# First stretch of a two-layer decoder trunk: the first column pair of x and its weights loaded in halves, the first split by halves of the tokens, fewer products of ones, another order of products

## The chip, the cores and the metric

The kernel runs on one core of one Trainium2 chip. The metric is the device time of one execution in microseconds (us), as the median of several runs.

Engines are named as the profile names them. PE is TensorE, the matrix engine, and PEld its weight loader, which puts the stationary operand of each product into the array. DVE is VectorE, ACT is ScalarE, POOL is GpSimd. SP is SyncE, which here only issues DMA transfers. SBUF is the on-chip memory from which the engines read; PSUM is the memory into which PE writes.

## The reference, cut to what matters

The program is two decoder layers over 512 tokens of width 1024, in 32-bit floats: attention with a short convolution in the first, gated linear attention in the second, each with a gated MLP and a per-layer embedding. The change lies in the first 20 us, where the first layer's input projection begins:

```python
h = _rms_norm(x, mix_norm[i])
q, k, v, cb, cc, cx = _split(h @ w_in, HY_SPLITS)      # 512, 128, 128, 512, 512, 512 columns
q = _apply_rope(_rms_norm(q.reshape(b, s, ATTN_Q_HEADS, HEAD_DIM), q_norm), cos, sin)
k = _apply_rope(_rms_norm(k.reshape(b, s, ATTN_KV_HEADS, HEAD_DIM), k_norm), cos, sin)
```

Keys and values together are 256 columns of `w_in` (512 to 767). They are the first products that the kernel makes.

## The kernel before

**Products in three.** PE multiplies 32-bit operands in a rounded form (fp32r). To keep precision each operand is split in two: ACT rounds it to a high part (lines 112 and 146), and DVE subtracts that from the original for the low part (lines 113 and 147). `mm3` (lines 166 to 168) makes high times high, high times low and low times high. So every product needs ACT's result first and then DVE's, and three matmuls on PE.

**The first stretch** is the start of `mixer0`. Activations are worked on transposed: features on the 128 partitions, tokens along the row. The 1024 features are eight blocks of 128, called columns here, m or k = 0 to 7. For each column PE transposes four blocks of 128 x 128, one for each group of 128 tokens t (line 477), into a 512-wide PSUM tile (`ps`). ACT and DVE read that tile, multiply it with the gain of the norm (the column `vec`) and split it into an operand pair (`operand`, lines 112 and 113). They also copy the plain tile into `xT[m]` for later (`keep`, line 492: even columns on ACT, odd ones on DVE). The weights of keys and values for two columns at a time are split by `weight` (lines 146 and 147, 512 wide). `keys_values(k)` then makes twelve products 256 columns wide: four token groups times the three of `mm3`, added up in two PSUM tiles (`pa`) over k = 0 to 7.

**Loads.** SP issues, for each of four pairs of columns, two transfers of x (256 tokens by 256 columns each, 256 KB, into `xin[0]` and `xin[1]`, line 441) and one of the weights (256 KB into `kvr`, line 442), one after another. ACT issues the identity matrix and the gains of the norms (lines 191 and 217). POOL's transfers come later: they wait for the last column of x to land.

**Products of ones.** `idle(n)` (line 202) makes n products of a matrix of ones, 512 columns wide, whose result goes nowhere. There are seven ahead of the first transposes, and three between the first transposes and the first product. Between the first transposes stands one more small product, which turns the gains of the norm into columns (line 226; DVE copies them out, line 227).

**What sets the order.** Around the change, PE, DVE and ACT follow the order in which the code is written (`manual_schedule`); each engine works its own list strictly in that order, and an instruction that waits holds up everything behind it on its engine. Behind that stretch a scheduler orders the instructions. The order in the code is: transposes of columns 0 and 1, products of ones, weights 0, operands 0 and 1, products of k = 0; then for c = 1 to 3: transposes of columns 2c and 2c + 1, the two copies into xT for the pair before, the operands and weights of this pair, and the products of k = c. The products of k = 4 to 7 follow. After them come the products of the queries, 512 wide (lines 166 to 168 into `ps`), whose weights are loaded by SP and split by ACT and DVE 1024 wide.

Of the kernel before, what the change touches and what calls it, by code (L numbers as in the profile page):

```python
# [18 lines left out]
P = 128  # L19
S = 512  # L20
D = 1024
NT = S // P
ND = D // P
# [33 lines left out]
class Kernel:  # L57
# [121 lines left out]
    def setup(self):  # L179
        nc, a = self.nc, self.a  # L180
        self.mhalf = self.cp.tile([P, 32], F32, name="mhalf")[:, :16]
        self.cf = self.cp.tile([P, P + 64 + 256], F32, name="cf")
        self.ident = self.cf[:, :P]
        ones = self.sq()[:, :P]
        self.ones_r = self.cp.tile([P, P], F32R, name="ones_r")
        self.nowhere = self.pa()
        with self.tc.manual_schedule(engines={ET.PE, ET.DVE, ET.Activation}):
            nc.vector.memset(ones, 1.0)
            nc.vector.tensor_copy(self.ones_r, ones)
            nc.vector.memset(self.mhalf, -0.5)  # L190
            nc.scalar.dma_start(self.ident, a["cst_f"][:, :P])
            self.vec0 = self.load_vectors0()
            self.idle(7)
        self.ones = self.ones_r.bitcast(F32)
        self.invf = self.cf[:, P + 32 : P + 64]
        self.amask = self.cf[:, P + 64 :]
# [233 lines left out]
    def mixer0(self):  # L430
        nc, a, tc = self.nc, self.a, self.tc
        with tc.tile_pool(name="m0", bufs=1) as mp:
            w_in = a["hy_w_in"][0].rearrange("(k p) n -> p k n", p=P)
            self.xT = [self.xp.tile([P, S], F32, name=f"xT{m}") for m in range(ND)]
            xin = [mp.tile([P, 2, D], F32, tag="s", name=f"xin{u}", bufs=2) for u in range(2)]
            kvr = self.raw(ND, 256)
            for c in range(4):
                cols = slice(c * 256, (c + 1) * 256)
                for u in range(2):
                    rows = a["x"][0, u * 256 : (u + 1) * 256, cols]  # L440
                    nc.sync.dma_start(xin[u][:, :, cols], rows.rearrange("(t p) d -> p t d", p=P))
                nc.sync.dma_start(kvr[:, 2 * c : 2 * c + 2, :], w_in[:, 2 * c : 2 * c + 2, 512:768])
            self.gate = xin[1][:, 1, D - 1 :]
            self.late(self.cf[:, P + 32 : P + 33])
            nc.gpsimd.dma_start(self.cf[:, P + 32 :], a["cst_f"][:, P:])
# [1 line left out]
            xg = self.xg = []  # L447
            tok = lambda k, t: (xg[k][0][:, t * P : (t + 1) * P], xg[k][1][:, t * P : (t + 1) * P])
            pkv = [self.pa() for _ in range(2)]
            pkv = [pkv[t // 2][:, (t % 2) * 256 : (t % 2) * 256 + 256] for t in range(NT)]  # L450
            wkv = []

            def keys_values(k):
                for t in range(NT):
                    self.mm3(
                        pkv[t], tok(k, t), wkv[k // 2](k % 2, 0, 256),
                        start=k == 0 and t % 2 == 0, stop=k == ND - 1 and t % 2 == 1,
                    )

            def first_keys_values():  # L460
                mm = nc.tensor.matmul
                wh, wl = wkv[0](0, 0, 256)
                for t in range(NT):
                    xh, _ = tok(0, t)
                    mm(pkv[t], xh, wh, start=t % 2 == 0, stop=False)
                    mm(pkv[t], xh, wl, start=False, stop=False)
                for t in range(NT):
                    mm(pkv[t], tok(0, t)[1], wh, start=False, stop=False)

            def turned_in(c):  # L470
                pss = [self.ps() for _ in range(2)]
                for u in range(2):
                    if c == 0 and u == 1:
                        self.vec0()
                    for m, ps in zip((2 * c, 2 * c + 1), pss):
                        for t in (2 * u, 2 * u + 1):
                            nc.tensor.transpose(
                                ps[:, t * P : (t + 1) * P], xin[u][:, t % 2, m * P : (m + 1) * P], self.ident
                            )
                return pss  # L480

            def weight(c):
                wkv.append(self.cut(kvr[:, 2 * c : 2 * c + 2, :], "a", (48, 16)))

            def operand(m, ps):
                hl = self.pair(self.fp, "a0", "a1")
                self.split(hl, ps, self.g_mix[0][:, m : m + 1])
                xg.append(hl)

            def keep(c, pss):  # L490
                return [
                    copy(self.xT[2 * c + u], pss[u]) for u, copy in enumerate((nc.scalar.copy, nc.vector.tensor_copy))
                ]

            with tc.manual_schedule(engines={ET.PE, ET.DVE, ET.Activation}):
                pss = turned_in(0)
                self.idle(3)
                weight(0)
                for u in range(2):
                    operand(u, pss[u])  # L500
                first_keys_values()
                for c in range(1, 4):
                    ahead = turned_in(c)
                    keep(c - 1, pss)
                    pss = ahead
                    operand(2 * c, pss[0])
                    weight(c)
                    operand(2 * c + 1, pss[1])
                    keys_values(c)
                last = keep(3, pss)  # L510
                for k in range(4, ND):
                    keys_values(k)
            wq = [self.weights(w_in[:, k0 : k0 + 4, :512], 4, 512, by="a") for k0 in (0, 4)]
            sums = self.few(NT, "ss")
            junk = mp.tile([P, D], F32, tag="pT", name="junk")
# [174 lines left out]
            pss = {}  # L690
# [4 lines left out]
            def conv_w(nme, j2):  # L695
                c0 = starts[nme] + 256 * j2
                return self.weights(w_in[:, :, c0 : c0 + 256], ND, 256)

            def conv_halves(nme, j2, *ins):
                c0 = starts[nme] + 256 * j2  # L700
                raw = self.raw(ND, 256)
                nc.sync.dma_start(raw, w_in[:, :, c0 : c0 + 256])
                ws = []

                def half(*ins):
                    c = slice(len(ws) * P, len(ws) * P + P)
                    with ExitStack() as es:
                        for x in ins:
                            es.enter_context(tc.issue_after(x))
                        ws.append(self.cut(raw[:, :, c], "b"))  # L710

                half(*ins)
                return (lambda k, a, b: ws[a // P](k, 0, P)), half
# [36 lines left out]
            w = conv_w("x", 0)  # L750
# [4 lines left out]
            w = conv_w("c", 0)  # L755
# [9 lines left out]
            w, second = conv_halves("b", 0, copied["q", 1])  # L765
# [7 lines left out]
            w, second = conv_halves("x", 1, copied[0, 1], begun[1])  # L773
# [9 lines left out]
            w, second = conv_halves("c", 1, copied[1, 1], begun[2])  # L783
# [5 lines left out]
            w, second = conv_halves("b", 1, copied[2, 1], begun[3])  # L789
# [1372 lines left out]
```

## Time and profile before

| | |
|---|---|
| Median of 3 runs | 1194.47 us (1193.74 to 1194.7) |
| Profiled execution, its own time | 1194.58 us |
| Its span, from the first to the last recorded instruction | 1192.8 us |
| Instructions | 17964 |
| Busy: PE, DVE, ACT, POOL | 1187.1, 994.6, 685.4, 43.1 us |
| DMA | 117.62 MB, mean 99 GB/s |

The profile is one execution of the program, recorded by the chip. A row of its timeline gives the start and the duration in us, the engine, the line of the code, the operation, what it writes and reads, the shapes and, in brackets, how long the engine sat idle just before and what released it. A matmul's recorded duration contains the way through the array. Matmuls overlap in it, so PE's pace is read from the distance between two starts, not from the durations. A transfer's "us to landing" counts from its issue. Names such as `wh`, `wl`, `a`, `ps`, `pa` are tiles: the high and the low part of the weights, the operands, the two kinds of PSUM tile.

### The profile page before, as it was taken

Reading aid. Unit: us, or ns where it says so; the run is one execution under the profiler, and the core shown is the slowest. Engines: PE = TensorE matmul, PEld = TensorE weight load, DVE = VectorE, ACT = ScalarE, POOL = GpSimd, SP = SyncE. Lnnn points to the kernel's source line nnn. Section 1 sums busy time; section 2 is a strip of 40 time slices with the busy share of each in tenths; the row PEclk is TensorE's granted clock in tenths of the full one; section 3 lists DMA queues with packets and bytes.
Section 4 is the critical chain, followed back from the end, with each engine's and each line's share of the span. In section 5 each row is a group of like instructions: output and inputs, shape, how many; then the busy total and the mean of one; then the engine's idle time right before and its main releaser. Section 6 shows DMA issues by size and latency. Waiting matters only on the chain.

```text
span 1192.8 us, 17964 instructions
## 1 busy us (share of the span) xinstructions
PE 1187.1 (100%) x7121; PEld 1038.9 (87%) x7121; DVE 994.6 (83%) x1571; ACT 685.4 (57%) x1116; POOL 43.1 (4%) x64
## 2 busy tenths in 40 slices
PE   9999999999999999999999999999999999999998
PEld 8887789999998889989988988889999999899887
DVE  6787687899999987789779866687999999986895
ACT  7566465655565744566563654555555656644764
POOL 2600000000000000000100000000000000000000
PEclk9999999999999999999999999999999999999999
DMA  7213322424232333232412222323242423423601
GB/s 224 82 62 91 90 71 71 142 71 142 71 118 95 119 129 98 97 106 70 142 60 71 74 69 71 107 65 112 72 141 71 142 72 122 135 89 98 212 1 71
DMA packets 110856, 117.62 MB, mean 99 GB/s; under 512 B 2824, under 2 KB 105794, under 8 KB 110772
## 3 DMA queue, kind: packets, MB, share of 16 engines
q1 hardware_dynamic: 109936, 115.88, 29.8%
q8 instruction: 56, 0.92, 0.3%
q0 software_dynamic: 560, 0.42, 0.3%
q14 instruction: 28, 0.23, 0.1%
q10 hardware_dynamic: 276, 0.18, 0.1%
HBM read 114.37 MB, written 2.10 MB: 98 GB/s over the span
## 4 chain that ended last, share of the span: by engine, by line
PE 100%; DVE 0%; ACT 0%; issue 0%
PE ps L166 14%; PE ps L167 14%; PE ps L168 14%; PE pa L167 7%; PE pa L166 7%; PE pa L168 7%; PE ps L912 6%; PE ps L914 6%; PE ps L913 6%; PE pa L912 2%; PE pa L914 2%; PE pa L913 2%; PE ps L1527 1%; PE ps L1526 1%; PE ps L1525 1%; PE pa L1866 1%
## 5 line engine op out<-in xcount | busy, mean ns | idle before, releaser
L146 ACT ACTIVATE wh<-raw 128x1024 fp32r<-128x1024 f32 (+4 forms) x144 | 143.6, 999 | 94.9 <-PE ps L167 61.7
L147 DVE TENSOR_TENSOR wl<-raw,wh 128x1024 fp32r<-128x1024 f32 (+4 forms) x144 | 166.0, 1153 | 28.9 <-ACT wh L146 28.1
L857 ACT ACTIVATE wh<-raw 128x1024 fp32r<-128x1024 f32 x84 | 89.3, 1063 | 119.6 <-DVE raw L881 63.8
L972 DVE SCALAR_TENSOR_TENSOR zt<-z,vfa,zt 128x510 f32<-128x510 f32 (+1 forms) x176 | 131.1, 747 | 5.3 <-ACT zt L970 4.7
L858 DVE TENSOR_TENSOR wl<-raw,wh 128x1024 fp32r<-128x1024 f32 x84 | 102.8, 1224 | 19.7 <-ACT wh L857 19.6
L970 ACT ACTIVATE zt<-z,vfb 128x512 f32<-128x512 f32 x88 | 71.0, 809 | 21.8 <-DVE four L1023 8.3
L166 PE MATMUL ps<-b,wh 128*128 128x512 f32 x192 | 76.2, 397 | 0.0
L167 PE MATMUL ps<-b,wh 128*128 128x512 f32 x192 | 75.0, 390 | 0.0
L168 PE MATMUL ps<-b,wl 128*128 128x512 f32 x192 | 74.9, 390 | 0.0
L912 PE MATMUL ps<-four,wh 128*128 128x256 f32 x256 | 71.5, 279 | 0.0
L914 PE MATMUL ps<-four,wl 128*128 128x256 f32 x256 | 71.0, 277 | 0.0
L913 PE MATMUL ps<-four,wh 128*128 128x256 f32 x256 | 70.8, 277 | 0.0
L167 PE MATMUL pa<-b,wh 128*128 128x512 f32 x176 | 69.0, 392 | 0.0
L167 PE MATMUL pa<-a,wh 128*128 128x512 f32 x176 | 69.0, 392 | 0.0
L166 PE MATMUL pa<-a,wh 128*128 128x512 f32 x176 | 69.0, 392 | 0.0
L166 PE MATMUL pa<-b,wh 128*128 128x512 f32 x176 | 69.0, 392 | 0.0
L168 PE MATMUL pa<-b,wl 128*128 128x512 f32 x176 | 68.4, 389 | 0.0
L168 PE MATMUL pa<-a,wl 128*128 128x512 f32 x176 | 68.4, 389 | 0.0
L166 PE MATMUL ps<-a,wh 128*128 128x512 f32 x128 | 50.6, 396 | 0.0
L167 PE MATMUL ps<-ul,wh 128*128 128x512 f32 x128 | 50.1, 391 | 0.0
L166 PE MATMUL ps<-uh,wh 128*128 128x512 f32 x128 | 50.1, 391 | 0.0
L912 PEld LDWEIGHTS ps<-four,wh 128*128 128x128 f32 x256 | 48.0, 188 | 2.3 <-ACT ps L937 0.5
(496 smaller groups left out, 3595.5 us busy)
## 6 DMA issues: line engine op xcount, KB each, us to landing
raw<-in_ffn_w_up_dram SPq DMA_DIRECT2D x44, 1024.0 KB, 5.1
raw<-in_ffn_w_down_dram SPq DMA_DIRECT2D x12, 1024.0 KB, 5.2
raw<-in_hy_w_in_dram SPq DMA_DIRECT2D x8, 1024.0 KB, 5.1
raw<-in_gla_w_in_dram SPq DMA_DIRECT2D x8, 1024.0 KB, 5.2
raw<-in_ffn_w_down_dram SPq DMA_DIRECT2D x8, 768.0 KB, 4.4
raw<-in_ple_w_gate_dram SPq DMA_DIRECT2D x6, 1024.0 KB, 5.2
raw<-in_hy_w_out_dram SPq DMA_DIRECT2D x16, 256.0 KB, 4.0
zt<-in_ffn_w_down_dram SPq DMA_DIRECT2D x8, 512.0 KB, 3.5
```

The source lines that it names most:

```text
L146: nc.scalar.activation(hv, v, AF.Copy)
L147: self.rest = nc.vector.tensor_tensor(lv, v, hv.bitcast(F32), ALU.subtract)
L166: mm(out, lh, rh, start=start, stop=False, **kw)
L167: mm(out, lh, rl, start=False, stop=False, **kw)
L168: return mm(out, ll, rh, start=False, stop=stop, **kw)
L857: nc.scalar.activation(h, src, AF.Copy)
L858: nc.vector.tensor_tensor(l, src, h.bitcast(F32), ALU.subtract)
L912: mm(out, wh, xh, start=first and j == 0, stop=False, **kw)
L913: mm(out, wh, xl, start=False, stop=False, **kw)
L914: mm(out, wl, xh, start=False, stop=j == ND // 2 - 1, **kw)
L970: nc.scalar.activation(y, z, AF.Identity, scale=w2[:, f : f + 1], bias=bb[:, f : f + 1])
L972: nc.vector.scalar_tensor_tensor(out=y[:, tap:], in0=z[:, : S - tap], scalar=w[:, f : f + 1], in1=y[:, tap:], op0=ALU.mult, op1=ALU.add,)
```

## The change

- The loads of columns 0 and 1 come apart: the chunks are columns 0, 1, 2 to 3, 4 to 5 and 6 to 7. SP issues 15 transfers instead of 12; the first six have 128 KB each.
- The weights are split by the same chunks: 256 wide for k = 0 and k = 1, and 512 wide from then on.
- Six products of ones stand ahead of the first transposes instead of seven, and one behind them instead of three.
- Only column 0 is transposed at first. Its operand is split in two halves of 256 tokens, with the split of its weights in between. The twelve products of k = 0 are ordered so that those of the first half of the tokens come first and those with the low part of the weights later.
- Column 1 is transposed behind the products of k = 0; its operand and weights follow.
- The transposes of the next pair of columns stand in the middle of a `keys_values`, behind its first six products. The products of 2c and of 2c + 1 both follow in round c, where before round c made those of k = c alone.

```diff
-            self.idle(7)
+            self.idle(6)
...
-            for c in range(4):
-                cols = slice(c * 256, (c + 1) * 256)
+            for k0, k1 in ((0, 1), (1, 2), (2, 4), (4, 6), (6, 8)):
+                cols = slice(k0 * P, k1 * P)
...
-                nc.sync.dma_start(kvr[:, 2 * c : 2 * c + 2, :], w_in[:, 2 * c : 2 * c + 2, 512:768])
+                nc.sync.dma_start(kvr[:, k0:k1, :], w_in[:, k0:k1, 512:768])
...
-            def keys_values(k):
+            def keys_values(k, then=None):
                 for t in range(NT):
                     self.mm3(
-                        pkv[t], tok(k, t), wkv[k // 2](k % 2, 0, 256),
+                        pkv[t], tok(k, t), wkv[k](0, 0, 256),
                         start=k == 0 and t % 2 == 0, stop=k == ND - 1 and t % 2 == 1,
                     )
+                    if then and t == 1:
+                        then()
...
-                for t in range(NT):
-                    xh, _ = tok(0, t)
-                    mm(pkv[t], xh, wh, start=t % 2 == 0, stop=False)
-                    mm(pkv[t], xh, wl, start=False, stop=False)
-                for t in range(NT):
-                    mm(pkv[t], tok(0, t)[1], wh, start=False, stop=False)
...
+                products((0, 1), 0, wh)
+                products((0, 1), 1, wh)
+                products((2, 3), 0, wh)
+                products(range(NT), 0, wl)
+                products((2, 3), 1, wh)
...
             with tc.manual_schedule(engines={ET.PE, ET.DVE, ET.Activation}):
-                pss = turned_in(0)
-                self.idle(3)
-                weight(0)
-                for u in range(2):
-                    operand(u, pss[u])
+                (ps0,) = turned_in((0,))
+                self.idle(1)
+                hl = self.pair(self.fp, "a0", "a1")
+                xg.append(hl)
+                half = [slice(0, S // 2), slice(S // 2, S)]
+                part = lambda c: self.split([x[:, c] for x in hl], ps0[:, c], self.g_mix[0][:, :1])
+                part(half[0])
+                weight(0, 1)
+                part(half[1])
                 first_keys_values()
+                (ps1,) = turned_in((1,))
+                keep(0, ps0)
+                operand(1, ps1)
+                weight(1, 2)
+                ahead = []
+                keys_values(1, lambda: ahead.extend(turned_in((2, 3))))
+                keep(1, ps1)
                 for c in range(1, 4):
-                    ahead = turned_in(c)
-                    keep(c - 1, pss)
-                    pss = ahead
+                    pss, ahead = ahead, []
                     operand(2 * c, pss[0])
-                    weight(c)
+                    weight(2 * c, 2 * c + 2)
                     operand(2 * c + 1, pss[1])
-                    keys_values(c)
-                last = keep(3, pss)
-                for k in range(4, ND):
-                    keys_values(k)
+                    if c < 3:
+                        keys_values(2 * c, lambda: ahead.extend(turned_in((2 * c + 2, 2 * c + 3))))
+                    else:
+                        keys_values(2 * c)
+                    last = [keep(2 * c + u, pss[u]) for u in range(2)]
+                    keys_values(2 * c + 1)
```

The order on PE from the last products of k = 0 to the first of k = 1, before. A row names the line, the operation, the tile written, the tiles read and the width; `ps_172` and `ps_173` take the transposes of columns 2 and 3, and `a_16` and `a_17` are the operand pair of column 1:

```order
L468 MATMUL pa_129<-wh_148,a_15_153 128x256 x2
L477 MATMUL ps_172<-cf,xin_111 128x128 x2
L477 MATMUL ps_173<-cf,xin_111 128x128 x2
L477 MATMUL ps_172<-cf,xin_112 128x128 x2
L477 MATMUL ps_173<-cf,xin_112 128x128 x2
L166 MATMUL pa_128<-wh_148,a_16_156 128x256
L167 MATMUL pa_128<-wl_149,a_16_156 128x256
L168 MATMUL pa_128<-wh_148,a_17_157 128x256
```

The same place now; `ps_165` takes the transposes of column 1, and `a_16` and `a_17` are its operand pair, made from `ps_165`; `wh_175` and `wl_176` are its own weights:

```order
L468 MATMUL pa_131<-wh_147,a_12_144 128x256 x2
L484 MATMUL ps_165<-cf,xin_110 128x128 x2
L484 MATMUL ps_165<-cf,xin_111 128x128 x2
L166 MATMUL pa_130<-wh_175,a_16_171 128x256
L167 MATMUL pa_130<-wl_176,a_16_171 128x256
L168 MATMUL pa_130<-wh_175,a_17_172 128x256
L166 MATMUL pa_130<-wh_175,a_16_171 128x256
L167 MATMUL pa_130<-wl_176,a_16_171 128x256
L168 MATMUL pa_130<-wh_175,a_17_172 128x256
L484 MATMUL ps_185<-cf,xin_110 128x128 x2
```

Before, the transposes ahead of the products of k = 1 were those of columns 2 and 3, whose operands were used one k later; now they are those of column 1 itself.

The order on DVE over the same stretch, before (line 113 makes low parts of operands, 147 low parts of weights, 492 copies to `xT`):

```order
L147 TENSOR_TENSOR wl_149<-raw_113,wh_148 128x512
L113 TENSOR_SCALAR a_15_153<-ps_132,vec_5_91,a_14_152 128x512
L113 TENSOR_SCALAR a_17_157<-ps_133,vec_5_91,a_16_156 128x512
L492 COPY xT_104<-ps_133 128x512
L113 TENSOR_SCALAR a_21_185<-ps_172,vec_5_91,a_20_184 128x512
L147 TENSOR_TENSOR wl_189<-raw_113,wh_188 128x512
```

And now:

```order
L113 TENSOR_SCALAR a_12_144<-ps_134,vec_5_91,a_11_143 128x256
L147 TENSOR_TENSOR wl_148<-raw_112,wh_147 128x256
L113 TENSOR_SCALAR a_12_144<-ps_134,vec_5_91,a_11_143 128x256
L113 TENSOR_SCALAR a_17_172<-ps_165,vec_5_91,a_16_171 128x512
L147 TENSOR_TENSOR wl_176<-raw_112,wh_175 128x256
L499 COPY xT_103<-ps_165 128x512
L113 TENSOR_SCALAR a_23_203<-ps_185,vec_5_91,a_22_202 128x512
L147 TENSOR_TENSOR wl_207<-raw_112,wh_206 128x512
```

The first operand's low part comes in two halves around the low part of its weights, and the low part of the weights of k = 1 stands behind the low part of the operand of column 1. Behind this stretch the engines' lists are the same apart from the places of a few small instructions in the first 60 of DVE and ACT and of one on PE.

More of the change, by code (lines that the diff above doesn't have):

```diff
@@ L451, in mixer0, with products, turned_in @@
             wkv = []
-            def keys_values(k):
+            def keys_values(k, then=None):
                 for t in range(NT):
                     self.mm3(
-                        pkv[t], tok(k, t), wkv[k // 2](k % 2, 0, 256),
+                        pkv[t], tok(k, t), wkv[k](0, 0, 256),
                         start=k == 0 and t % 2 == 0, stop=k == ND - 1 and t % 2 == 1,
                     )
+                    if then and t == 1:
+                        then()
             def first_keys_values():
-                mm = nc.tensor.matmul
                 wh, wl = wkv[0](0, 0, 256)
-                for t in range(NT):
-                    xh, _ = tok(0, t)
-                    mm(pkv[t], xh, wh, start=t % 2 == 0, stop=False)
-                    mm(pkv[t], xh, wl, start=False, stop=False)
-                for t in range(NT):
-                    mm(pkv[t], tok(0, t)[1], wh, start=False, stop=False)
-            def turned_in(c):
-                pss = [self.ps() for _ in range(2)]
+                started = set()
+                def products(ts, part, w):
+                    for t in ts:
+                        nc.tensor.matmul(pkv[t], tok(0, t)[part], w, start=t % 2 == 0 and t not in started, stop=False)
+                        started.add(t)
+                products((0, 1), 0, wh)
[3 more added lines that the diff above has]
+                products((2, 3), 1, wh)
+            def turned_in(ms):
+                pss = [self.ps() for _ in ms]
                 for u in range(2):
-                    if c == 0 and u == 1:
+                    if ms[0] == 0 and u == 1:
                         self.vec0()
-                    for m, ps in zip((2 * c, 2 * c + 1), pss):
+                    for m, ps in zip(ms, pss):
                         for t in (2 * u, 2 * u + 1):
@@ L480, in turned_in, with weight @@
                 return pss
-            def weight(c):
-                wkv.append(self.cut(kvr[:, 2 * c : 2 * c + 2, :], "a", (48, 16)))
+            def weight(k0, k1):
+                get = self.cut(kvr[:, k0:k1, :], "a", (48, 16))
+                wkv.extend(lambda i, c0, c1, k=k: get(k - k0, c0, c1) for k in range(k0, k1))
             def operand(m, ps):
@@ L488, in operand, with keep @@
                 xg.append(hl)
[L490 to L493, printed above, removed]
+            def keep(m, ps):
+                return (nc.vector.tensor_copy if m % 2 else nc.scalar.copy)(self.xT[m], ps)
             with tc.manual_schedule(engines={ET.PE, ET.DVE, ET.Activation}):
-                pss = turned_in(0)
-                self.idle(3)
-                weight(0)
-                for u in range(2):
-                    operand(u, pss[u])
-                first_keys_values()
+                (ps0,) = turned_in((0,))
[7 more added lines that the diff above has]
+                part(half[1])
+                first_keys_values()
+                (ps1,) = turned_in((1,))
[5 more added lines that the diff above has]
+                keep(1, ps1)
                 for c in range(1, 4):
-                    ahead = turned_in(c)
-                    keep(c - 1, pss)
-                    pss = ahead
+                    pss, ahead = ahead, []
                     operand(2 * c, pss[0])
-                    weight(c)
+                    weight(2 * c, 2 * c + 2)
                     operand(2 * c + 1, pss[1])
-                    keys_values(c)
-                last = keep(3, pss)
-                for k in range(4, ND):
-                    keys_values(k)
+                    if c < 3:
[4 more added lines that the diff above has]
+                    keys_values(2 * c + 1)
             wq = [self.weights(w_in[:, k0 : k0 + 4, :512], 4, 512, by="a") for k0 in (0, 4)]
```

## The prediction

> **What bounds the kernel now.** I read the busy shares first, then the stretches around the change, then the waits of PE and its weight loader, and last the timeline of the first 22 us, where every edit lies. First row: busy time by engine for the whole span. Next three: busy time by stretch (start:end, length, then PE, PEld, DVE, ACT, POOL). Last: what PE itself waited for in the whole run.
>
> ```profile
> PE 1187.1 (100%) x7121; PEld 1038.9 (87%) x7121; DVE 994.6 (83%) x1571; ACT 685.4 (57%) x1116; POOL 43.1 (4%) x64
> ...
> 0.00:8.00 8.00, 6.69 (x22) 5.29 (x23) 2.16 (x7) 3.47 (x6) 0.34 (x6) 1.00 0.76 232
> 8.00:22.00 14.00, 14.00 (x121) 13.85 (x120) 11.27 (x18) 12.23 (x20) 6.82 (x17) 1.00 0.89 269
> ...
> PE pa L202 <- DVE mhalf L190: 1.3, 1, 1.3
> ```
>
> PE sets the end. After its first 1.3 us it waits for nobody, so what delays or advances PE in the first stretch arrives at the end nearly undiminished. The question is only when the last product of keys and values ends, and with it the first product of the queries begins. Now the timeline (start, duration, engine, line, what):
>
> ```profile
> 3.62 0.33 PEld L202 LDWEIGHTS pa<-ones_r 128*128 128x128 f32 x1
> 4.05 0.22 PEld L477 LDWEIGHTS ps<-cf,xin 128*128 128x128 f32 x1
> 4.47 1.05 PE L477 MATMUL ps<-cf,xin 128*128 128x128 f32 x4
> 5.45 0.28 PE L226 MATMUL pa<-cf,vrow 16*128 16x16 f32 x1
> 5.77 0.63 ACT L146 ACTIVATE wh<-raw 128x512 fp32r<-128x512 f32 x1 [2.54 <-DMA raw<-in_hy_w_in_dram]
> 5.77 0.17 DVE L227 COPY vec<-pa 128x16 f32<-128x16 f32 x1 [4.49 <-PE pa L226]
> 6.15 0.63 PE L477 MATMUL ps<-cf,xin 128*128 128x128 f32 x2
> 6.36 0.42 PE L477 MATMUL ps<-cf,xin 128*128 128x128 f32 x1
> 7.01 0.61 PE L202 MATMUL pa<-ones_r 128*128 128x512 f32 x1
> 7.69 0.28 PE L465 MATMUL pa<-wh,a 128*128 128x256 f32 x1
> 7.81 0.28 PE L466 MATMUL pa<-wl,a 128*128 128x256 f32 x1
> 9.09 1.03 PE L477 MATMUL ps<-cf,xin 128*128 128x128 f32 x8
> 9.88 0.36 PE L166 MATMUL pa<-wh,a 128*128 128x256 f32 x1
> 9.94 0.69 ACT L112 ACTIVATE a<-ps,vec 128x512 fp32r<-128x512 f32 x1 [1.45 <-PE ps L477]
> 10.53 0.62 ACT L146 ACTIVATE wh<-raw 128x512 fp32r<-128x512 f32 x1
> 10.66 0.75 DVE L113 SCALAR_TENSOR_TENSOR a<-ps,vec,a 128x512 fp32r<-128x512 f32 x1 [1.54 <-ACT a L112]
> 11.33 0.68 DVE L147 TENSOR_TENSOR wl<-raw,wh 128x512 fp32r<-128x512 f32 x1
> ...
> 14.46 0.36 PE L166 MATMUL pa<-wh,a 128*128 128x256 f32 x1
> 16.21 1.06 ACT L146 ACTIVATE wh<-raw 128x1024 fp32r<-128x1024 f32 x1
> 18.21 1.22 DVE L147 TENSOR_TENSOR wl<-raw,wh 128x1024 fp32r<-128x1024 f32 x1
> 21.50 0.28 PE L168 MATMUL pa<-wh,a 128*128 128x256 f32 x1
> ```
>
> Three readings. **PE's pace**: products of ones follow each other by 0.43 us (loads at 3.62 and 4.05) and transposes by 0.21 (6.15, 6.36); from about 7.4 on a transpose takes 0.10 (eight from 9.09 to 9.88) and a 256-column product 0.119 (sixty start from 14.46 to 21.50). The pace doubles near 7.4 us, although the column of the granted clock says 1.00 everywhere. **The operand chain**: m2's last transpose is the sixth of the group at 9.09, so it starts at 9.59; ACT takes it up at 9.94, 0.35 later. ACT starts the weights' high part 0.59 behind, DVE the low part of the operand 0.72 behind, and the low part of the weights 0.67 after that, for 0.68. From the sixth transpose to a complete operand pair is 0.35 + 0.72 + 0.67 + 0.69 = 2.43 us. **Why nobody waits for it now**: the chain for m2 ends at 12.01, but from 9.88 PE has the twelve products of k = 1 and the next eight transposes, and comes to k = 2 at 12.17. One k of products always stands between an operand's transposes and its use.
>
> **What the change takes away in front.** One of seven products of ones: PE's loader comes to the first transposes at 3.62 instead of 4.05, PE at 4.04. They need only column 0 now. The first landings:
>
> ```profile
> xin<-in_x_dram SPq DMA_DIRECT2D x2, 256.0 KB, 3.4
> cf<-in_cst_f_dram ACTq DMA_DIRECT2D x1, 64.0 KB, 3.0
> ...
> raw<-in_hy_w_in_dram SPq DMA_DIRECT2D x1, 256.0 KB, 4.0
> ...
> 0.73 0.95 SPq L441 DMA_DIRECT2D xin<-in_x_dram  x2
> 1.73 0.46 SPq L442 DMA_DIRECT2D raw<-in_hy_w_in_dram  x1
> ```
>
> The second x transfer, issued near 1.2, landed at 4.6 with 256 KB; with 128 KB it lands between 1.2 + 3.0 (the 64 KB row) = 4.2 and 4.6, and it is needed at 4.8. The first weights land between 1.73 + 3.0 = 4.7 and, as now, 1.73 + 4.0 = 5.73; needed at 5.5. I take the middle, 5.2, so no wait; the upper end costs 0.2. The gain column's transfer has no landing on record; PE used it at 5.45, so it may come after the 4.60 of the next paragraph, for 0.5 at most (a rival). The same issuing queue now has 15 transfers where it had 12, at about 0.48 each, but the first six are half as long, and the later chunks are wanted later than now (below), so I cost the three issues at nothing. If the DMA served rows of 512 bytes no faster than rows of 1 KB, all landings would be as now; that is a rival.
>
> The Trainium skill, DMA: Bandwidth & Descriptors, Specifications, gives 512 bytes as the least transfer for line rate. By that the halved rows (128 floats) are just long enough and the landings follow the bytes, which gives the sum below; the 64 KB row here, also of 512-byte rows, cannot tell the two apart.
>
> Two slow transposes from 4.04; the product with the gain column 0.35 after the last one (now 5.10 to 5.45), so at 4.60; DVE's copy done 0.49 later, 5.09. ACT's high part of the first token half: 256 columns are not in the trace. From 512 and 1024 columns (0.62 and 1.06 on ACT, 0.68 and 1.22 on DVE) half a tile saves 0.22 on ACT and 0.27 on DVE: 0.47 and 0.40 for ACT's two kinds, 0.48 and 0.41 for DVE's. As bounds stand the full durations above and half of them below. So high half 5.1 to 5.6, wh to 5.95, the first product at about 6.05 instead of 7.69. Its followers are ready in time: low half 6.1, second high half (which the order puts behind the first low half) 6.6, wl 6.5, second low half 7.1. Twelve products: at 0.21 until 7.4, the rest at 0.12, end at 8.1. Before, PE stood there at 9.09: **1.0 us gained**, of the 1.6 by which the first product moves, since seven of them run at the slow pace.
>
> **What it adds behind.** At 8.1 PE has transposed only m0; m1's four transposes come now, 0.4 us, until 8.5. Then k = 1 is next on PE with nothing between. The last of the four starts at 8.4. ACT takes m1 up at 8.75 (its copy of x to xT stands ahead, but is over by 7.7), wh is done at 8.75 + 0.59 + 0.40 = 9.74, the low part starts at 9.47, wl at 10.14 and ends at 10.55. PE's first product goes at 9.8, its second needs wl and waits until 10.65. Behind it on PE stand all products and the transposes of m2 and m3, so everything waits. **First stall: 8.5 to 10.65 less one product, 2.0 us.**
>
> The rest of k = 1 with the eight transposes in its middle takes 11 x 0.119 + 0.79 + 0.1 for the change of kind = 2.2, to 12.85. But m2's sixth transpose starts at 10.65 + 5 x 0.119 + 0.05 + 0.5 = 11.8, and the whole pair for k = 2 (now full-sized weights) is there at 11.8 + 2.43 = 14.2. **Second stall: to 14.3, less the one product that needs only high parts, 1.35 us.** From here two k share a chunk: PE reaches the second product of k = 4 at 14.3 + 2.2 + 12 x 0.119 + 0.12 = 18.05; the chain for it ends at 14.3 + 0.65 + 0.5 + 2.43 = 17.9. No third stall, by 0.1 to 0.2; likewise k = 6. ACT and DVE have 2.6 and 2.8 us of work per chunk against PE's 3.7, so they keep up.
>
> The last product ends at 17.93 + 0.89 + 48 x 0.119 = 24.5 us; now it ends at 21.50 + 0.12 = 21.6. The sum: -1.0 + 0.4 + 2.0 + 1.35 and 0.15 for one more change of kind = **+2.9 us**. The query weights are split behind the last copy to xT: ACT from 21.7 for 1.06, DVE until 24.1, wanted at 24.75, so 0.6 is left. Their second chunk's transfer, held back until the kv weights' buffer is free (near 21.5 instead of 17.07), has until 35 us.
>
> The profiled execution took 1194.58 us with a span of 1192.8; 2.9 more is 1197.5. The median shown lies 0.1 lower: **1197.4 us**.
>
> **Bounds.** Landings: 0 to +0.5. Half-size DVE splits: wl of k = 1 alone counts, 0.34 to 0.68 against 0.41, so -0.1 to +0.3. Hand-overs 0.05 longer or shorter in each of eight links of the two stalls: -0.4 to +0.4. The doubling of the pace at 6.1 instead of 7.4: -0.45. The likeliest case alone spans +2.0 to +3.9, 1196.5 to 1198.4.
>
> **Rivals.**
>
> *The slow pace lasts.* The first stretch had ten products of ones, now seven, and PE idles 3.4 us before 14.3. If the pace doubles only after the first stall, five products cost 0.09 more and four transposes 0.11 more: 0.9, to 1198.3. If it also falls back over the stalls, the twelve products and eight transposes of k = 1 add about 2 more less what the second stall hides of it: 1199.7. For it: the trace shows the slow pace as long as PE had only ones and transposes. Against: PE does as much before 7.4 as now.
>
> The Trainium skill, TensorE: Matmul & The Clock Gate, Parts 1 and 4, holds that the clock opens after a busy window of about 3.4 us whose phase is not tied to the program, that an idle window closes it, and that transposes do not count as busy. The late doubling agrees with it (7.4 us); by its window, stalls of 2.0 and 1.35 us, each with work beside it, would not close the clock.
>
> *The halves land no earlier,* and the gain column, whose landing is not on record, not before 5.45. The column is then 0.85 later, the first product near 6.9; of the twelve only three are slow, so they end at 8.6, 0.5 later, and the stalls follow unshortened: 1197.9. For it: twice as many rows for the same bytes of x. Against: PE found the first x transfer landed at 4.05, and small transfers here land in 3.0.
>
> *The delay is taken back later (the other side).* The loader's waits after the stretch:
>
> ```profile
> PEld ps L678 <- issue: 2.9, 10, 0.4
> PEld pa L661 <- ACT s L655: 0.8, 1, 0.8
> PEld pa L661 <- ACT cxs L727: 0.8, 1, 0.8
> PEld pa L661 <- issue: 0.8, 1, 0.8
> ```
>
> If ACT and DVE reached the softmax around 70 to 120 us at their old times while PE comes 2.9 us late, these 5.3 us of loader waits could shrink by up to 2.9, back to 1194.5. It decides once 0.5 us comes back. Against it: that work starts from the queries' products, which move along, and PE itself shows no wait there.
>
> A gain has a ceiling: even without any stall the first product moves by 1.6 us, under 0.2%.
>
> **Chances.** Likeliest case 0.66, slow pace 0.17, late landings 0.08, taken back 0.09. A measurement of this kernel tells about 0.2%, 2.4 us, from no change, so slower begins at 1196.9. A sixth of the likeliest case lies under that, 0.11; with 0.06 of the taken-back case, no change has 0.17. Faster has 0.03, the rest of that case. Slower: 0.55 + 0.17 + 0.08 = 0.80. The range leaves out about 0.1 on each side: 1196.2 to 1199.9.
>
> **What would show it.** In the new timeline: the first product near 6.1; m1's transposes near 8.1; a hole on PE from about 8.5 to 10.6 released by ACT and then DVE's wl, and one from 12.9 to 14.3; none of size afterwards; the first 512-column product of the queries near 24.7 instead of 21.86. Products 0.2 apart after 8 us would show the slow pace, a first product at 7 or later the landings. The forecast is wrong if the holes are under half as long, or if the queries start 2.9 late and the end is not.

## The result, and the profile after

| | before | with the change |
|---|---|---|
| Median of 7 runs | 1194.47 us | 1197.83 us |
| Lowest to highest | 1193.74 to 1194.95 | 1197.61 to 1200.77 |
| Span of the profiled execution | 1192.8 us | 1196.0 us |

The ratio of the times is 1.0031, with a 95% interval of 1.0022 to 1.0040. The change makes the kernel 3.4 us slower; 1197.4 was forecast.

The page of the changed kernel, busy time by engine, and after it what PE itself waited for in the whole run (who waited for whom, us in total, times, longest):

```profile
PE 1187.2 (99%) x7118; PEld 1037.7 (87%) x7118; DVE 994.3 (83%) x1573; ACT 685.7 (57%) x1118; POOL 43.5 (4%) x64
...
PE pa L166 <- ACT wh L146: 1.4, 2, 1.1
PE pa L202 <- DVE mhalf L190: 1.3, 1, 1.3
PE pa L167 <- DVE wl L147: 0.9, 2, 0.5
PE pa L468 <- ACT wh L146: 0.5, 1, 0.5
```

The work is the same: PE is busy for 1187.2 us where it was 1187.1. What grew is the span around it. Before, PE had one wait, at the start; now it has five more, all in the first 15 us. Each recorded wait is shorter than the loss, since a matmul's record (0.28 us and more) runs on beyond the next start (0.12 us later); the distance between starts shows the loss. The timeline of the changed kernel:

```profile
4.04 0.63 PE L484 MATMUL ps<-cf,xin 128*128 128x128 f32 x2
4.60 0.28 PE L226 MATMUL pa<-cf,vrow 16*128 16x16 f32 x1
5.54 0.47 ACT L112 ACTIVATE a<-ps,vec 128x256 fp32r<-128x256 f32 x1 [2.31 <-PE ps L484]
8.14 0.61 PE L484 MATMUL ps<-cf,xin 128*128 128x128 f32 x4
8.78 0.69 ACT L112 ACTIVATE a<-ps,vec 128x512 fp32r<-128x512 f32 x1 [0.60 <-PE ps L484]
9.37 0.41 ACT L146 ACTIVATE wh<-raw 128x256 fp32r<-128x256 f32 x1
9.50 0.75 DVE L113 SCALAR_TENSOR_TENSOR a<-ps,vec,a 128x512 fp32r<-128x512 f32 x1 [1.95 <-ACT a L112]
9.83 0.38 PE L166 MATMUL pa<-wh,a 128*128 128x256 f32 x1 [1.08 <-ACT wh L146]
10.17 0.42 DVE L147 TENSOR_TENSOR wl<-raw,wh 128x256 fp32r<-128x256 f32 x1
10.64 0.38 PE L167 MATMUL pa<-wl,a 128*128 128x256 f32 x1 [0.43 <-DVE wl L147]
13.45 0.39 PE L166 MATMUL pa<-wh,a 128*128 128x256 f32 x1 [0.37 <-ACT wh L146]
13.58 0.71 DVE L147 TENSOR_TENSOR wl<-raw,wh 128x512 fp32r<-128x512 f32 x1
14.35 0.38 PE L167 MATMUL pa<-wl,a 128*128 128x256 f32 x1 [0.51 <-DVE wl L147]
24.57 0.39 PE L166 MATMUL ps<-wh,a 128*128 128x512 f32 x1
```

Two holes are to be read here. From the four transposes of column 1, at 8.14, PE does one product until 10.64; the steps of ACT and DVE that release it stand in the rows between. The same happens ahead of k = 2, until 14.35. After that no hole: the queries start at 24.57. Before, they started here:

```profile
21.86 0.50 PE L166 MATMUL ps<-wh,a 128*128 128x512 f32 x1
```

And the last output transfer, issued by SP when all work is done, before and now:

```profile
1189.94 0.33 SPq L1572 DMA_DIRECT2D out_dram<-so  x1
```

```profile
1192.80 0.33 SPq L1589 DMA_DIRECT2D out_dram<-so  x1
```

It is issued 2.86 us later. The span grew by 3.2, so the last 0.3 us lies in the landing of that transfer.

### The profile page after: what moved, and what is told of

Its sections match the earlier page's. It is cut to its first block, busy times and chain, and to the rows that moved or that the text cites. A ratio compares the mean times of both kernels' runs of the same rounds, so it can differ in the third digit from the quotient of the medians.

```text
span 1196.0 us, 17965 instructions
## 1 busy us (share of the span) xinstructions
PE 1187.2 (99%) x7118; PEld 1037.7 (87%) x7118; DVE 994.3 (83%) x1573; ACT 685.7 (57%) x1118; POOL 43.5 (4%) x64
## 4 chain that ended last, share of the span: by engine, by line
PE 99%; ACT 0%; DVE 0%; issue 0%
PE ps L166 14%; PE ps L167 14%; PE ps L168 14%; PE pa L167 7%; PE pa L166 7%; PE pa L168 7%; PE ps L929 6%; PE ps L931 6%; PE ps L930 6%; PE pa L929 2%; PE pa L931 2%; PE pa L930 2%; PE ps L1544 1%; PE ps L1542 1%; PE ps L1543 1%; PE pa L1883 1%
## 5 line engine op out<-in xcount | busy, mean ns | idle before, releaser
L146 ACT ACTIVATE wh<-raw 128x1024 fp32r<-128x1024 f32 (+5 forms) x145 | 143.6, 993 | 91.5 <-PE ps L167 59.9
L147 DVE TENSOR_TENSOR wl<-raw,wh 128x1024 fp32r<-128x1024 f32 (+5 forms) x145 | 165.2, 1141 | 26.0 <-ACT wh L146 25.1
L166 PE MATMUL ps<-a,wh 128*128 128x512 f32 x128 | 50.6, 395 | 0.0
L167 PE MATMUL ps<-a,wh 128*128 128x512 f32 x128 | 50.0, 390 | 0.0
```

Source lines behind the costliest of these rows:

```text
L146: nc.scalar.activation(hv, v, AF.Copy)
L147: self.rest = nc.vector.tensor_tensor(lv, v, hv.bitcast(F32), ALU.subtract)
L166: mm(out, lh, rh, start=start, stop=False, **kw)
L167: mm(out, lh, rl, start=False, stop=False, **kw)
```

## Experiments

The theory: the operands of k = 1 and k = 2 are begun too late for PE, and the two waits for them cost more than the new front gains. The rivals: the loads in halves cost the time, or PE's slow pace does, for want of products of ones. Each ratio is against runs of the kernel before in the same comparison (median 1194.94 us for the first four, 1194.76 for the next four, 1195.01 for the last). The diffs are against the changed kernel.

**1. Column 1 earlier.**

```diff
                 part(half[1])
-                first_keys_values()
                 (ps1,) = turned_in((1,))
-                keep(0, ps0)
                 operand(1, ps1)
                 weight(1, 2)
+                keep(0, ps0)
+                first_keys_values()
```

> The change, but column 1 is transposed ahead of the products of k = 0 and its operand and weights are split ahead of the copy of column 0. The operand chain theory: the operands and weights of k = 1 are then ready at 8.8 us instead of 10.6, so the first stall shrinks from 2.0 us to some 0.4; the second, ahead of k = 2, stays at 1.3. About 1196.0 us, 1.8 below the change. Rival, the halved loads or the slow pace cost the time: no gain, 1197.8.

Measured: 1196.14 us, ratio 1.0008 (0.9999 to 1.0016); 1.2 above before. PE's waits and starts ahead of k = 1 and k = 2, and the queries:

```profile
8.79 0.39 PE L167 MATMUL pa<-wl,a 128*128 128x256 f32 x1 [0.23 <-DVE wl L147]
11.61 0.38 PE L166 MATMUL pa<-wh,a 128*128 128x256 f32 x1 [0.37 <-ACT wh L146]
12.48 0.39 PE L167 MATMUL pa<-wl,a 128*128 128x256 f32 x1 [0.48 <-DVE wl L147]
22.70 0.39 PE L166 MATMUL ps<-wh,a 128*128 128x512 f32 x1
```

The second product of k = 1 starts at 8.79 instead of 10.64, the queries 1.87 earlier. About 1.5 of that is the stall, of which 0.5 is left; 0.4 is the time of the four transposes, which now stand where PE idled ahead of its first product. The second stall is untouched.

**2. Columns 2 and 3 earlier.**

```diff
-                keys_values(1, lambda: ahead.extend(turned_in((2, 3))))
+                ahead.extend(turned_in((2, 3)))
+                keys_values(1)
```

> The change, but columns 2 and 3 are transposed ahead of the products of k = 1 instead of in their middle, so in the first stall, where PE idles. The operand chain theory: the pair for k = 2 is ready at 12.5 us instead of 14.3, the first stall stays, the second shrinks to some 0.4. About 1196.0 us, 1.8 below the change. Rival, the halved loads or the slow pace: no gain, 1197.8.

Measured: 1196.31 us, ratio 1.0013 (1.0004 to 1.0022). Now the first stall stays and the second goes:

```profile
10.64 0.38 PE L167 MATMUL pa<-wl,a 128*128 128x256 f32 x1 [0.43 <-DVE wl L147]
12.49 0.38 PE L167 MATMUL pa<-wl,a 128*128 128x256 f32 x1 [0.18 <-DVE wl L147]
22.72 0.39 PE L166 MATMUL ps<-wh,a 128*128 128x512 f32 x1
```

The queries start 1.85 earlier than with the change. About 1.0 of that is the second stall (1.3 with the change, 0.3 here); 0.9 is the time of the eight transposes, which now stand in the first hole. The two stalls are separate costs, and each all but goes when its own transposes move; loads, splits in halves and products of ones stayed as they were.

**3. The old front under the new order.**

```diff
-            self.idle(6)
+            self.idle(7)
...
-            for k0, k1 in ((0, 1), (1, 2), (2, 4), (4, 6), (6, 8)):
+            for k0, k1 in ((0, 2), (2, 4), (4, 6), (6, 8)):
...
-                self.idle(1)
...
-                part(half[0])
+                self.idle(3)
                 weight(0, 1)
-                part(half[1])
+                operand(0, ps0)
```

> The new order of transposes and products, with the old front: loads of columns 0 and 1 in pairs (12 transfers), seven and three products of ones, operand 0 in one piece, products of k = 0 in three groups of four. The operand chain theory: both stalls as in the change; k = 0 ends near 8.6 us instead of 8.1, so about 1198.3 us, 0.5 above the change. Rival, the halved loads or fewer products of ones cost the time: back to near 1194.5.

Measured: 1199.15 us, ratio 1.0039 (1.0026 to 1.0051), with single executions from 1197.58 to 1202.66. So neither the halved loads nor the missing products of ones made the loss. In the profile, of the shortest execution, both stalls stand at the same places (second products at 10.65 and 14.33). One expectation missed: the products of k = 0 end not near 8.6 but here,

```profile
8.16 0.60 PE L482 MATMUL ps<-cf,xin 128*128 128x128 f32 x4
```

0.02 behind the change's 8.14, in an execution whose pace had doubled by 5.4. So this profile shows no gain of the halves themselves; with a pace that doubled near 4.9 the new front ends at 7.91 and 7.88 (experiments 7 and 9), so they bring some 0.3 at most when the pace is early. The highest executions were not profiled, and what made them long stays open. The two highest have a mean granted clock of 0.997 and 0.998 on record, the other four 0.999 or more, so a lower clock may have had a part in them. The change's own longest, 1200.77, has 1.000.

**4. The new front with the old order behind it.**

```diff
+                (ps1,) = turned_in((1,))
+                operand(1, ps1)
+                weight(1, 2)
                 first_keys_values()
...
                 for c in range(1, 4):
-                    pss, ahead = ahead, []
+                    ahead = turned_in((2 * c, 2 * c + 1))
+                    for u in range(2):
+                        keep(2 * c - 2 + u, pss[u])
+                    pss = ahead
...
+                    keys_values(c)
+                last = [keep(6 + u, pss[u]) for u in range(2)]
+                for k in range(4, ND):
+                    keys_values(k)
```

> The new front (loads in halves, one operand in two halves, six and one products of ones), but the old order behind it: columns 0 and 1 transposed ahead of the first product, the pair 2c and 2c + 1 ahead of the products of k = c, the products of k = 4 to 7 last. The operand chain theory: no stall after the first product, and k = 0 ends near 8.2 us instead of 9.1 with the same work done; transposes of columns 4 to 7 may wait 0.2 for their loads. About 1193.8 us, 0.7 below before. Rival, the front itself costs: at or above 1194.5.

Measured: 1194.95 us, ratio 1.0000 (0.9991 to 1.0009). With the old order the stalls are gone and so is the loss, to within the 1 us that the interval leaves. The front's gain came out smaller than expected:

```profile
3.74 0.95 SPq L441 DMA_DIRECT2D xin<-in_x_dram  x2
8.31 0.60 PE L484 MATMUL ps<-cf,xin 128*128 128x128 f32 x4
9.20 0.66 PE L484 MATMUL ps<-cf,xin 128*128 128x128 f32 x4 [0.29 <-DMA xin<-in_x_dram]
21.59 0.50 PE L166 MATMUL ps<-wh,a 128*128 128x512 f32 x1
```

The products of k = 0 end at 8.31 instead of 9.09, but the queries start only 0.27 earlier, at 21.59 instead of 21.86. PE is early enough to meet the transfers of columns 2 and 3, and waits for the second token half, which landed at 9.15. Before, it had landed at 7.45. SP now issues these transfers behind three more than before, when they were issued here:

```profile
2.24 0.98 SPq L441 DMA_DIRECT2D xin<-in_x_dram  x2
```

**5 to 7. The change again, with its idle time filled, and with more products of ones.** The fifth is the change itself. The sixth has `self.idle(6)` behind `weight(1, 2)` and `self.idle(4)` ahead of `keep(1, ps1)`. The seventh has `self.idle(3)` for `self.idle(1)`.

> The change again, beside the next three and more often. The operand chain theory: 2.9 to 3.4 us above before, and a spread from execution to execution as that of before. Rival, the slow pace decides in part: single executions stand 1 to 5 us above the fastest, since in them PE's pace doubles later or falls back in the stalls.

> The change with six products of ones ahead of the products of k = 1 and four ahead of those of k = 2, where PE idles 2.0 and 1.3 us; they fill 1.4 and 0.9 us of it and lengthen nothing if the pace is the fast one. The operand chain theory: the same median as the change, within 0.3 us. Rival, the idle time itself lets the pace fall in some executions: the median falls by some tenths, and the executions 1 to 5 us above the fastest are gone.

> The change with three products of ones behind the first transposes, as before, instead of one. PE idles there from 5.6 to 6.4 us, so the two added ones at 0.43 each delay the first product by some 0.1 us. The operand chain theory: the same as the change, within 0.2 us, since the first stall ends with the weights of k = 1 whatever stands ahead. Rival, the removed ones cost the time through the pace: 0.5 to 3 us below the change.

Measured: 1198.25 us (ratio 1.0030, 1.0019 to 1.0042), 1198.95 (1.0034, 1.0021 to 1.0046) and 1198.30 (1.0030, 1.0019 to 1.0040). The change comes out 3.5 above before, 0.1 more than expected. Filling the idle time lowers nothing, and its executions spread from 1197.74 to 1200.45, no narrower than the change's own 1197.58 to 1199.29 beside them. The sixth was expected within 0.3 of the change and lies 0.7 above it. The intervals overlap, and in its profile the queries start at 24.54, as with the change; PE falls behind by 0.9 only near 834 us, in a wait for ACT. The two products of ones bring nothing back. So the slow pace does not make the loss. The spread has at least one other source, far behind the change; the first row is from the fifth run, the second from the profile of the change, for the same split of weights:

```profile
238.94 1.06 ACT L146 ACTIVATE wh<-raw 128x1024 fp32r<-128x1024 f32 x1 [0.54 <-DMA raw<-in_ffn_w_up_dram]
```

```profile
238.18 1.05 ACT L146 ACTIVATE wh<-raw 128x1024 fp32r<-128x1024 f32 x1
```

There a weight transfer landed late, ACT waited for it, and PE behind it: its next product starts at 240.33 instead of 239.93. Both executions had started the queries within 0.02 us of each other, and their spans differ by 0.6, of which this is 0.4.

**8. An attempt at a version better than both.** Experiment 4 with each token half of column 0 in a PSUM tile of its own (its copy to `xT` then comes in two halves), and two transfers for column 1 issued by POOL. The diff shows what it adds to experiment 4:

```diff
-                    nc.sync.dma_start(xin[u][:, :, cols], ...
+                    q = nc.gpsimd if (k0, u) == (1, 1) else nc.sync
+                    q.dma_start(xin[u][:, :, cols], ...
...
+                (nc.gpsimd if k0 == 1 else nc.sync).dma_start(kvr[:, k0:k1, :], ...
...
-                (ps0,) = turned_in((0,))
+                ps0 = [self.ps(), self.ps()]
+                for u in range(2):
...
+                        nc.tensor.transpose(ps0[u][:, t * P : (t + 1) * P], xin[u][:, t % 2, :P], self.ident)
```

> The new front with the old order behind it (as e4), and two things more: the two token halves of column 0 are transposed into PSUM tiles of their own, and the transfers of column 1's weights and of its second token half are issued by POOL, so that SP comes to columns 2 and 3 some 1.0 us sooner. If the wait of 0.29 us for columns 2 and 3 in e4 comes from SP's issues, it goes; if the first half's split waited for the second half's transposes because they share a PSUM tile, it starts at 5.1 us instead of 5.54 and the first product near 6.0 instead of 6.43. Together the queries start near 21.1 us: 0.5 below e4, 0.6 to 0.8 below before. Rival: no gain over e4.

Measured: 1194.55 us, ratio 0.9998 (0.9989 to 1.0007): no difference from before that can be told. One expectation held, the first split starts early:

```profile
2.00 0.78 POOL L442 DMA_DIRECT2D xin<-in_x_dram  x1
2.24 1.48 SPq L442 DMA_DIRECT2D xin<-in_x_dram  x3
5.13 0.47 ACT L112 ACTIVATE a<-ps,vec 128x256 fp32r<-128x256 f32 x1 [1.91 <-DVE vec L227]
6.54 1.12 PE L485 MATMUL ps<-cf,xin 128*128 128x128 f32 x4 [0.61 <-DMA xin<-in_x_dram]
7.31 1.63 PE L469 MATMUL pa<-wh,a 128*128 128x256 f32 x6
8.73 1.05 PE L469 MATMUL pa<-wl,a 128*128 128x256 f32 x4
22.97 0.50 PE L166 MATMUL ps<-wh,a 128*128 128x512 f32 x1
```

Here the gain column released it, where with the change PE's transposes did, at 5.54. But PE waited 0.61 for column 1, and the products then ran 0.21 apart. The transfers of the two token halves of column 1, POOL's issued at 2.00 and SP's at 2.24:

```profile
xin<-in_x_dram POOLq DMA_DIRECT2D x1, 128.0 KB, 4.4
xin<-in_x_dram SPq DMA_DIRECT2D x1, 128.0 KB, 4.3
```

The transposes at 6.54 began when SP's half landed, at 6.5, though SP issued it as early as in experiment 4, where they began at 5.73. POOL's half landed at 6.4, 4.4 after its issue; with the change SP's transfer of that half took 2.9. So with two transfers moved to POOL, SP's own came late as well. Why, no run here shows.

**9. The weights ahead of the operands on ACT and DVE.** PE's order is untouched.

```diff
                 (ps1,) = turned_in((1,))
+                weight(1, 2)
                 keep(0, ps0)
                 operand(1, ps1)
-                weight(1, 2)
...
+                weight(2, 4)
                 keep(1, ps1)
+                operand(2, ahead[0])
                 for c in range(1, 4):
                     pss, ahead = ahead, []
-                    operand(2 * c, pss[0])
-                    weight(2 * c, 2 * c + 2)
+                    if c > 1:
+                        operand(2 * c, pss[0])
+                        weight(2 * c, 2 * c + 2)
```

> The change, but the weights of k = 1 are split ahead of the copy of column 0 and of operand 1, and those of k = 2 and 3 ahead of the copy of column 1 and of operand 2; nothing moves on PE. The operand chain theory: each stall then ends with the low part of the operand, not with that of the weights behind it; PE waits at its third product, until 10.3 us instead of 10.64 at the second, and for k = 2 until 13.25 instead of 14.35. About 1.2 us below the change, 2.0 above before. Rival, the chain's order on ACT and DVE plays no part: as the change, 3.3 above before.

Measured: 1197.42 us, ratio 1.0022 (1.0013 to 1.0030).

```profile
10.04 0.38 PE L168 MATMUL pa<-wh,a 128*128 128x256 f32 x1 [0.29 <-DVE a L113]
13.00 0.39 PE L168 MATMUL pa<-wh,a 128*128 128x256 f32 x1 [0.29 <-DVE a L113]
23.11 0.39 PE L166 MATMUL ps<-wh,a 128*128 128x512 f32 x1
```

The waits moved from the second product (line 167, for `wl`) to the third (line 168, for the low part of the operand), as the chain says. The median is 2.4 above before, where 2.0 was expected. In the profile the queries start 1.46 earlier than with the change. Of this 0.3 comes from the front, since PE ran at the fast pace from 4.8 us on here (both waits end some 0.25 earlier than expected); 1.2, as expected, comes from the order on ACT and DVE.

**10 and 11. POOL for the weights of column 1 alone; and the eighth once more.** The tenth sets `q = nc.sync` throughout in the eighth.

> As e8, but column 1's second token half is issued by SP again; only its weights go through POOL. If the wait of 0.6 us at the transposes of column 1 in e8 came from POOL's transfer, it is gone, and SP still comes to columns 2 and 3 some 0.5 us sooner than in e4. The queries start near 21.3 us, about 0.5 below before. Rival: no gain over e4, as before within 0.2 us.

> e8 once more, for another profile. In e8's profile PE's pace doubled only near 10 us and the queries started at 22.97, 1.2 to 1.9 later than its fastest executions would allow. If the moment of the doubling differs from execution to execution of the same kernel, this one doubles at 7.4 or earlier and starts the queries near 21.1 to 21.4. Rival, the wait of 0.6 us ahead of the first product causes it: again near 10 us and 22.97.

The tenth: 1194.66 us, ratio 0.9999 (0.9990 to 1.0008). The wait for column 1 is down to under 0.1 us, but PE waits 0.58 us for columns 2 and 3 at 9.34, later than in experiment 4, though SP issued them about half a microsecond sooner. So SP's issue alone did not set their landing; what did stays open. The queries start at 21.73, where 21.3 was expected. The eleventh:

```profile
6.83 0.66 PE L485 MATMUL ps<-cf,xin 128*128 128x128 f32 x4 [1.39 <-DMA xin<-in_x_dram]
7.24 0.94 PE L469 MATMUL pa<-wh,a 128*128 128x256 f32 x6
8.02 0.63 PE L469 MATMUL pa<-wl,a 128*128 128x256 f32 x4
21.50 0.50 PE L166 MATMUL ps<-wh,a 128*128 128x512 f32 x1
```

The same kernel, a single execution of 1194.47 us, with the transposes of column 1 later still (6.83 instead of 6.54), but four products take 0.63 instead of 1.05 and the queries start 1.47 earlier. The wait does not make the slow pace: with a longer wait the pace was fast.

## Why the prediction was right

**The size and the cause.** The forecast stalls stand in the profile to within 0.05 us: the first product of k = 1 at 9.83 (forecast 9.8), its second at 10.64 (10.65); for k = 2, 13.45 (13.4) and 14.35 (14.3). By the distances between starts the stalls cost 1.95 (forecast 2.0) and 1.3 (1.35). There is no third stall, as computed. Experiments 1 and 2 take away most of one stall each, and the queries start 1.87 and 1.85 earlier; 9 shortens both by the order on ACT and DVE alone; 4 takes both away and has no loss.

**The front.** k = 0 was forecast to end at 8.1, and the next transposes start at 8.14. But two steps of that term were wrong and cancelled, so it is luck that it came out. The first high half was to start at 5.1; it started at 5.54, so the first product came at 6.37 instead of 6.05. Experiment 8 shows why: with both halves in one PSUM tile, ACT waited for the second half's transposes too. And the products were to run at the slow pace until 7.4; they ran at the fast one from the first, recorded at 0.28 to 0.39 each where the slow ones of experiment 8 have 0.41 and more. In the changed kernel the pace doubled between the product of ones at 5.15 and 6.37. At this pace the followers were not ready in time either; PE's weight loader waited for the high part of the second token half:

```profile
7.09 0.30 PEld L468 LDWEIGHTS pa<-wh,a 128*128 128x128 f32 x2 [0.19 <-ACT a L112]
```

The three more transfers that SP issues were costed at nothing. That holds for the change, which transposes columns 2 and 3 only at 11.34. In experiment 4, which comes to them at 8.31, the wait for them takes 0.5 of the 0.8 us that the front gains.

**Absorption.** Next to none, 0.1 us: the queries start 2.7 us later and, with the position transposes that stood ahead of them before and stand behind their fourth product now, 2.95 (their sixth product starts at 26.07 instead of 23.12); the output is issued 2.86 later.

**The remainder.** The medians differ by 3.4, the sum said 2.9. The profiled pair shows 0.3 of the rest in the landing of the last output transfer. Whether every execution has it the traces cannot say. The bounds listed with the sum add up to +4.1 at the upper end, not the +3.9 written there; 3.4 lies inside either.

**The rivals.** Halves that land no earlier: the second token half of x landed 2.6 us after its issue where the 256 KB had taken 3.4, so they did land earlier; the gain column landed at 3.7, and its product started at 4.60 as forecast. The slow pace: experiments 5 to 7 speak against it as the cause, and in every profile the record of the granted clock holds one unbroken stretch of full clock from the doubling to beyond PE's last product, so in none did the pace fall back in the stalls. A late doubling does exist, and in this change an early one gains little (in 7 the pace doubled at 4.9 us and the queries started only 0.27 sooner). For executions that were not profiled this stays open. Delay taken back: 0.1 us at most.

## What to carry to other kernels

Where one engine sets the end and follows a fixed order, ask of each group of its work how much of other work stands between the step that starts its operands and the step that uses them; here the chain over ACT and DVE takes 2.4 us, and before the change twelve products and the rest of the transposes just covered it. Moving a first product forward by 1.3 us is worth nothing if that cover is taken from the second. And a gain at the front ends at the next transfer: with the stalls removed, PE ran into the landing of the next columns, whose issue the cutting of the first loads had itself moved back.

## What the runs showed that was not expected

- PE's pace doubles at different moments: near 7.4 us before the change, between 5.2 and 6.4 with it, and in one and the same kernel between 4.3 and 4.8 (experiment 11) and after 10.0 (experiment 8); there the queries start 1.47 us later. It is the granted clock after all, though its column shows 1.00 everywhere: the traces' record of it begins, at full clock, where the distances between starts halve, at 7.47 us before the change, 5.73 with it, 4.58 in experiment 11 and 10.38 in 8. Ahead of that it has no entry, and the column counts this as 1.00. In all profiles the stretch of full clock lasts 1184.4, 1187.8 or 1191.3 us, in steps of 3.4 us. The Trainium skill, TensorE: Matmul & The Clock Gate, Part 1, says that the window behind this runs free of the program; the two profiles of one kernel agree. The page gives ±500 ns of spread between runs; here the two differ by over 5 us.
- A read of half a PSUM tile waited for PE's writes to the other half: 0.41 us, gone with two tiles (5.54 against 5.13). Whether the chip asks for that or only the way the program is ordered, no run here shows.
